# Output gates of a hybrid GLA/FNet layer: from channels on partitions to tokens on partitions, stored as 16-bit halves and reloaded by transposing transfers

## The chip, the cores and the metric

The kernel runs on one core of one Trainium2 chip. The metric is device time of one execution in microseconds (us): 1936.42 us is the median of 3 runs before the change (1936.19 to 1936.66). Engines are named as in the profile: PE (TensorE matmul), PEld (its weight loads), DVE (VectorE), ACT (ScalarE), POOL (GpSimd), SP (SyncE, which issues most DMAs).

## What is computed

One layer over 384 tokens (128 context, 256 latent) of width D = 2048, in float32. The part that matters here is the mixer:

```
def mixer(h, ...):
    proj = h @ w_in                      # q, k, v, g, decay factors, Fourier groups
    ...                                  # o: bidirectional gated linear attention (GLA)
    ...                                  # f: 2-D Fourier mixing
    gates = sigmoid(h @ w_gate + b_gate) # w_gate: 2048 x 4096
    g_a, g_b = split(gates, 2)
    merged = g_a * (o @ w_br_gla) + g_b * (f @ w_br_four)
    return merged @ w_out
```

Around it stand adaLN modulation (vectors from `w_ada`), RMSNorms and a SwiGLU FFN of 5632 hidden channels.

## The kernel before

All products keep float32 accuracy by splitting both operands in two parts of a shorter format (hi and lo) and summing three products: hi x hi, hi x lo, lo x hi. The activations stand as `hT` (tiles `A_hi`, `A_lo`): 16 blocks of 128 channels on partitions, 384 tokens along the row. Weights come in tiles of 128 x 1024 (512 KB): SP loads one into `raw` (two buffers), ACT casts it to `whi`, DVE subtracts to give `wlo` (four buffers of each). `load`, `split`, `push` and `grab` (L187 to L240) do that: each `grab` hands out the oldest ready tile, issues the load of a later one and the cast and split of the one loaded before. The order of the loads is the list `srcs` at the top.

The stages around the change, in the order of time:

- **Gates** (197 to 503 us). For each of 32 blocks of 128 gate channels `proj` (L259) takes two weight tiles; the weights stand in the array (stationary, 128 x 128) and the 384 tokens stream (moving): 48 matmuls of 384 columns into one PSUM tile `pmm` of the pool `psm` (three banks). `gate` (L839) evicts it with the bias to `gz` (ACT, L841) and stores it to DRAM as `gates_d[i]`, channels on partitions, tokens along the row. After each tile `step(sd)` runs one step of two side programs. One is `gla()`, a generator for the linear attention of four heads that goes on to its next `yield`. The other is `ada`, which streams `w_ada` through DVE (L574, two operations of 128 x 1024 per step) for the modulation vectors. Both put their work between the tiles of the main stream, on the same in-order engines. The GLA's small products use a pool of five other banks (`pss`).
- **Fourier inputs** (503 to 600 us): eight more blocks of `proj`, with `dft()` and `ada` in the side steps.
- **Merge** (600 to 761 us). The list `mix_order` interleaves eight projections for the GLA's own output gate ("o"), 16 Fourier products ("b", `four`) and 16 GLA products ("a"). A b unit takes one weight tile, whose halves DVE first adds and subtracts (`fold`, L204 and L205), then 17 short matmuls, evictions on ACT and DVE, a product with its gate and a store of y to DRAM (`four_d`). An a unit takes one tile, 24 matmuls of 384 columns, a product with its gate (L1033), the sum with the reloaded y and a split into the tiles of the next stage. Once the o units are over, a, b, a repeats. After each a or b unit `gate_of` (L962) loads the gate of a unit further on (`gates_d`, and y for a units) and applies the sigmoid to the gate of the next one (ACT, L977).
- Then the output projection, the residual and the FFN (from 761 us). In the FFN the 512-column form is used: tokens are the stationary operand, four blocks of 128 weight columns the moving one. That stage also turns tiles by splitting float32 in 16-bit halves (`apart`, L1610), transposing DMAs from ACT's queue (L1616) and joining the halves (`together`, L1620).

ACT, DVE, POOL and PE run in the order of the program. SP's order is set by the scheduler of the language, by priority.

Of the kernel before, what the change touches and what calls it, by code (L numbers as in the profile page):

```python
# [11 lines left out]
F32 = mybir.dt.float32  # L12
# [9 lines left out]
P = 128  # L22
# [75 lines left out]
def tile_step(ctx: ExitStack, tc: tile.TileContext, a, o):  # L98
# [48 lines left out]
    for i in range(XU, 8):  # L147
        srcs += two(a["w_in"], i)
    for i in range(32):
        srcs += two(a["w_gate"], i)  # L150
    for i in range(16, 24):
# [38 lines left out]
    def load(raw=None):  # L190
        n, src = next(srcs, (0, None))
        if src is not None:
            if raw is None:
                raw = wp.tile([P, G], F32, tag="raw", name="raw", bufs=2)
            SP.dma_start(raw, src)
            raws.append((raw, n in folded))
# [406 lines left out]

    gates_d = dram.tile([32, P, T], F32, name="gates_d")
    qT, kT = qk[:, 0:4, :], qk[:, 4:8, :]
# [8 lines left out]
    with ExitStack() as s:  # L614
# [23 lines left out]
        def gla():  # L638
# [10 lines left out]
            for h in range(NH):  # L649
# [9 lines left out]
                for d in range(2):  # L659
                    s0.append(pg.tile([P, 1, DV], F32, tag=f"s0{d}", name="s0"))  # L660
                    SP.dma_start(s0[d], a["s0"][d, h])
                yield
                qin, kin, kcr, kout, dec = [], [], [], [], []
# [86 lines left out]
                for c in range(2):  # L750
                    v = att[hf(c), :, c * CH : (c + 1) * CH]
                    DVE.tensor_add(v, v, am[hf(c)])
                yield
                for d in range(2):
# [82 lines left out]
        rate[0] = 1.0  # L837
        for i in range(32):
            def gate(p, i=i):  # L839
                g = pg.tile([P, T], F32, tag="gz", name="gz", bufs=2)  # L840
                ACT.activation(g, p, AF.Identity, bias=bgate[:, i : i + 1])  # L841
# [7 lines left out]
    four_d = dram.tile([KT, P, T], F32, name="four_d")  # L849
    with ExitStack() as s:  # L850
# [110 lines left out]

        def gate_of():  # L962

            u = next(gorder, None)
            if u is not None:
                b, i = u
                g = pc.tile([P, T], F32, tag="gate", name="gate", bufs=4)
                SP.dma_start(g, gates_d[i + (16 if b == "b" else 0)])
                y = None
                if b == "a":  # L970
                    y = pc.tile([P, T], F32, tag="yb", name="yb", bufs=4)
                    SP.dma_start(y, four_d[i])
                gates[u] = g, y
                raw_gates.append(g)
            if raw_gates and (u is None or len(raw_gates) > 1):
                g = raw_gates.pop(0)
                ACT.activation(g, g, AF.Sigmoid)  # L977

# [38 lines left out]
        for b, i in mix_order:  # L1017
            if b == "o":
                if i == 1:
                    gate_of()  # L1020
# [1002 lines left out]
```

## Time and profile before

| | |
|---|---|
| median of 3 runs | 1936.42 us |
| the profiled execution | 1936.08 us |
| its span, first to last instruction | 1934.3 us |
| PE, DVE, ACT busy | 99%, 85%, 55% |
| gates, from 197 to 503 us | 306 us |
| merge, from 600 to 761 us | 161 us |
| granted TensorE clock | 0.999 |

The profile is one execution taken by the hardware profiler. A row of a timeline gives the start, the duration, the engine, the source line, the operation, the tiles written and read, the shape and, in brackets, how long the engine stood idle before it and what ended that. A row of a group gives least, median and greatest duration in ns. In the windows the numbers are busy time and, in brackets, the count of each engine; the last three are the granted clock, the mean busy share of the 16 DMA engines and the GB/s that they moved. Matmuls overlap, so their durations are longer than their distance from start to start.

### The profile page before, as it was taken

How to read it: one execution, taken by the hardware profiler on the slowest of the kernel's cores; microseconds unless marked ns; L12 is line 12 of the kernel's file. 1: busy time of each engine (PE TensorE's matmuls, PEld its weight loads, DVE VectorE, ACT ScalarE, POOL GpSimd, SP SyncE). 2: the span in 40 equal slices, each digit the busy share in tenths (PEclk: the TensorE clock that was granted, in tenths of full speed). 3: DMA queues.
4: the chain of work that ended last, by engine and by line, in shares of the span. 5: the costliest groups of instructions: out<-in, count | busy, mean ns of one | idle time of the engine just before them, and what ended most of it. 6: DMA issues, size and time to landing. Idle time of an engine off the chain costs nothing.

```text
span 1934.3 us, 27954 instructions
## 1 busy us (share of the span) xinstructions
PE 1918.5 (99%) x10398; PEld 1702.5 (88%) x10398; DVE 1641.8 (85%) x2059; ACT 1069.3 (55%) x1523; POOL 145.2 (8%) x171
## 2 busy tenths in 40 slices
PE   8999999999999999999999999999999999999998
PEld 5779999999999999999988888888888888888886
DVE  5569888879776797977789999999999999988885
ACT  4233454554335655446556666766666666666555
POOL 0000000000000000002100111111111120211001
PEclk9999999999999999999999999999999999999999
DMA  9978676767754687654639696979788797969553
GB/s 389 371 263 269 228 257 219 241 219 259 256 190 145 204 287 246 218 185 154 231 98 280 155 284 151 262 170 244 191 243 207 212 230 192 252 136 253 158 199 128
DMA packets 246152, 429.12 MB, mean 222 GB/s; under 512 B 45308, under 2 KB 149948, under 8 KB 241664
## 3 DMA queue, kind: packets, MB, share of 16 engines
q1 hardware_dynamic: 199072, 386.70, 60.0%
q0 software_dynamic: 18432, 33.56, 11.3%
q10 hardware_dynamic: 28512, 7.08, 2.3%
q8 instruction: 81, 1.33, 0.3%
q14 instruction: 55, 0.45, 0.1%
HBM read 365.68 MB, written 54.53 MB: 217 GB/s over the span
## 4 chain that ended last, share of the span: by engine, by line
PE 97%; DMA 1%; DVE 1%; ACT 0%; issue 0%; SPq 0%; POOL 0%; DVEq 0%; POOLq 0%; ACTq 0%
PE pmm L257 36%; PE pgu L1539 31%; PE pdn L1539 10%; PE pds L1539 7%; PE pv L399 3%; PE pgm L382 1%; PE pf L998 1%; DMA slab<-in_w_ada 1%; PE px L417 1%; PE pmm L1253 1%; PE pf L999 1%; PE bk L1539 1%; PE po L647 1%; PE pr L582 0%; PE dl L647 0%; PE pp L881 0%
## 5 line engine op out<-in xcount | busy, mean ns | idle before, releaser
L257 PE MATMUL pmm<-A_hi,whi 128*128 128x384 f32 x1200 | 404.3, 337 | 0.0
L257 PE MATMUL pmm<-A_hi,wlo 128*128 128x384 f32 x1200 | 401.4, 334 | 0.0
L257 PE MATMUL pmm<-A_lo,whi 128*128 128x384 f32 x1200 | 401.3, 334 | 0.0
L1437 ACT CAST whi<-u 128x1024 fp32r<-128x1024 f32 x200 | 210.1, 1053 | 173.1 <-PE pds L1539 42.6
L223 ACT CAST whi<-raw 128x1024 fp32r<-128x1024 f32 x181 | 189.8, 1051 | 171.3 <-DMA raw<-in_w_gate 62.2
L1448 DVE TENSOR_TENSOR wlo<-u,whi 128x1024 fp32r<-128x1024 f32 x200 | 243.7, 1220 | 34.1 <-ACT whi L1437 32.5
L224 DVE TENSOR_TENSOR wlo<-raw,whi 128x1024 fp32r<-128x1024 f32 x179 | 217.9, 1220 | 52.5 <-ACT whi L223 49.7
L1539 PE MATMUL pgu<-whi,A_hi 128*128 128x512 f32 x640 | 249.9, 390 | 0.0
L1539 PE MATMUL pgu<-whi,A_lo 128*128 128x512 f32 x640 | 249.2, 389 | 0.0
L257 PEld LDWEIGHTS pmm<-A_hi,whi 128*128 128x128 f32 x1200 | 225.3, 188 | 2.9 <-issue 1.8
L257 PEld LDWEIGHTS pmm<-A_lo,whi 128*128 128x128 f32 x1200 | 225.4, 188 | 0.2
L257 PEld LDWEIGHTS pmm<-A_hi,wlo 128*128 128x128 f32 x1200 | 225.3, 188 | 0.0
L574 DVE SCALAR_TENSOR_TENSOR adacc<-adaw,cond,adacc 128x1024 f32<-128x1024 f32 x180 | 222.7, 1278 | 2.8 <-DMA adaw<-in_w_ada 2.5
L1437 ACT CAST whi<-raw 128x1024 fp32r<-128x1024 f32 x157 | 165.0, 1053 | 87.2 <-PE pgu L1539 27.9
L1448 DVE TENSOR_TENSOR wlo<-raw,whi 128x1024 fp32r<-128x1024 f32 x157 | 191.1, 1218 | 12.6 <-ACT whi L1437 12.2
L1539 PE MATMUL pgu<-wlo,A_hi 128*128 128x512 f32 x640 | 185.8, 389 | 0.0
L1539 PEld LDWEIGHTS pgu<-whi,A_hi 128*128 128x128 f32 x640 | 120.1, 188 | 25.9 <-issue 0.8
L1539 PEld LDWEIGHTS pgu<-wlo,A_hi 128*128 128x128 f32 x640 | 120.1, 188 | 25.1
L1539 PEld LDWEIGHTS pgu<-whi,A_lo 128*128 128x128 f32 x640 | 120.1, 188 | 24.7
L1539 PE MATMUL pgu<-whi,S 128*128 128x512 f32 x400 | 116.6, 389 | 0.0
L1672 POOL DMA_DIRECT2D sums_d<-spare x64 | 58.5, 950 | 625.3 <-ACT spare L1668 618.9
L1539 PE MATMUL pdn<-whi,hid_hi 128*128 128x512 f32 x264 | 102.8, 389 | 0.0
(410 smaller groups left out, 3302.3 us busy)
## 6 DMA issues: line engine op xcount, KB each, us to landing
adaw<-in_w_ada SPq DMA_DIRECT2D x96, 512.0 KB, 4.2
raw<-in_w_d SPq DMA_DIRECT2D x70, 512.0 KB, 5.2
slab<-in_w_ada SPq DMA_DIRECT2D x32, 1024.0 KB
raw<-in_w_gate SPq DMA_DIRECT2D x64, 512.0 KB, 4.5
raw<-in_w_g SPq DMA_DIRECT2D x48, 512.0 KB, 3.7
raw<-in_w_u SPq DMA_DIRECT2D x48, 512.0 KB, 5.2
raw<-in_w_in SPq DMA_DIRECT2D x44, 512.0 KB, 4.3
u<-in_w_u SPq DMA_DIRECT2D x40, 512.0 KB, 7.1
```

The costliest lines, as they stand in the source:

```text
L223: ACT.copy(hi, raw)
L224: sub = lambda: eng.tensor_sub(lo, raw, hi.bitcast(F32))
L257: PE.matmul(dst, w[wi][:, k * n + n0 : k * n + n0 + P], x[xi][:, k0 + k, :], start=first and k == 0 and j == 0, stop=last and k == kts - 1 ...
L382: PE.matmul(pgv[q : q + 32, :], spad[:, k, :], slab[k // (KT // 2)][:, k % (KT // 2), :], start=k < 4, stop=k >= KT - 4,)
L399: PE.matmul(pv[2 * t + g], hT[x_][:, kb, t * P : (t + 1) * P], w_[:, g * 512 : (g + 1) * 512], start=kb == 0 and j == 0, stop=kb == KT - 1 ...
L417: PE.matmul(px, w_[:, u * P : (u + 1) * P], hT[x_][:, kb, :], start=j == 0, stop=j == 2)
L574: DVE.scalar_tensor_tensor(acc[:, c, :], w, cond[:, k, c : c + 1], acc[:, c, :], op0=ALU.mult, op1=ALU.add,)
L647: PE.matmul(dst, w[wi], x[xi], start=first and j == 0, stop=last and j == 2)
L1437: ACT.copy(hi, src)
L1448: DVE.tensor_sub(lo, src, hi.bitcast(F32))
L1539: PE.matmul(dst, stat[x_][m], mov(w[w_], m), start=first and w_ == m == x_ == 0, stop=last and w_ == m == 1, skip_group_check=any(more),)
L1672: POOL.dma_start(sums_d[k], u, accum_op=ALU.add)
```

## The change

- **Matmuls of the gates.** Tokens become the stationary operand and 512 gate channels the moving one. A group q of 512 channels takes eight weight tiles m, each with 2 x 128 input channels for 512 gate channels (its load reads runs of 256 floats). Per tile there are 3 token tiles x 2 input blocks x 3 products = 18 matmuls of 512 columns. The group's result stands in three PSUM banks, one for each token tile, which are all that the pool `psm` has.
- **Eviction and store.** After tile m=7 of a group ACT copies each bank, read as 16-bit numbers, so that the 128 low halves and the 128 high halves of each channel block stand in rows of their own (`gpl`, three buffers), and SP stores it: tokens on partitions.
- **Reload.** In the merge a transposing DMA from SP's queue brings 256 of these 16-bit columns back as 128 channels x (2 halves x 384 tokens). ACT then joins the halves into `gate` (new copy, L1007) and applies the sigmoid, now with the bias (L1010). Reloads are issued four units ahead (`gate_load`), y as before.
- **Side steps.** `gla()` loses three of its yields per head: after the loads of the initial states, after the merge of the attention masks, and after the output product of token tile 0. At m=6 and m=7 of each group only `ada` is stepped.
- `gates_d` becomes eight DRAM tensors and `four_d` sixteen.

```diff
-    for i in range(32):
-        srcs += two(a["w_gate"], i)
+    for q in range(8):
+        for m in range(8):
+            src = a["w_gate"][4 * q : 4 * q + 4, m // 4, :, 256 * (m % 4) : 256 * (m % 4) + 256]
+            srcs.append(src.rearrange("n p x -> p n x"))
...
                     SP.dma_start(s0[d], a["s0"][d, h])
-                yield
...
                     DVE.tensor_add(v, v, am[hf(c)])
-                yield
...
                     ACT.activation(junk, po, AF.Square, accum_out=ss[:, t, h : h + 1])
-                    yield
+                    if t:
+                        yield
...
-        for i in range(32):
-            def gate(p, i=i):
-                g = pg.tile([P, T], F32, tag="gz", name="gz", bufs=2)
-                ACT.activation(g, p, AF.Identity, bias=bgate[:, i : i + 1])
-                SP.dma_start(gates_d[i], g)
-
-            proj(psm, hT, gate, sd)
+        for q in range(8):
+            pt = [psm.tile([P, 512], F32, tag="mm", name="pgt") for _ in range(3)]
+            for m in range(8):
+                w = [x.rearrange("p (n k c) -> p n k c", n=4, k=2) for x in grab()]
+                for t in range(3):
+                    ts = slice(t * P, (t + 1) * P)
+                    for k in range(2):
+                        for j, (wi, xi) in enumerate(((0, 0), (0, 1), (1, 0))):
+                            PE.matmul(
+                                pt[t], hT[xi][:, 2 * m + k, ts], w[wi][:, :, k, :],
+                                start=m == k == j == 0, stop=m == 7 and k == 1 and j == 2,
+                            )
+                    if m == 7:
+                        pl = pg.tile([P, 2 * 512], U16, tag="gpl", name="gpl", bufs=3)
+                        ACT.copy(
+                            pl.rearrange("p (n h c) -> p n h c", n=4, h=2),
+                            pt[t].bitcast(U16).rearrange("p (n c h) -> p n h c", n=4, h=2),
+                        )
+                        SP.dma_start(gates_d[q][ts, :], pl)
+                step(ada if m in (6,7,) else sd)
...
+        def gate_load():
+
+            u = next(gorder, None)
+            if u is not None:
+                b, i = u
+                n = i + (16 if b == "b" else 0)
+                pl = pc.tile([P, 2 * T], U16, tag="gpl", name="gpl", bufs=4)
+                SP.dma_start(
+                    pl.rearrange("p (h t) -> p h t", h=2), gates_d[n // 4][:, 256 * (n % 4) : 256 * (n % 4) + 256],
+                    transpose=True,
+                )
+                raw_gates.append((u, pl))
...
+        def gate_of():
+
+            if raw_gates:
+                u, pl = raw_gates.pop(0)
+                b, i = u
+                n = i + (16 if b == "b" else 0)
+                g = pc.tile([P, T], F32, tag="gate", name="gate", bufs=3)
+                y = ys.pop(u, None)
+                y_load()
+                ACT.copy(
+                    g.bitcast(U16).rearrange("p (x h) -> p h x", h=2), pl.rearrange("p (h x) -> p h x", h=2),
+                )
+                ACT.activation(g, g, AF.Sigmoid, bias=bgate[:, n : n + 1])
                 gates[u] = g, y
-                raw_gates.append(g)
-            if raw_gates and (u is None or len(raw_gates) > 1):
-                g = raw_gates.pop(0)
-                ACT.activation(g, g, AF.Sigmoid)
+            gate_load()
```

Three places show what moves in the engines' own order. ACT among the gates, before, in the first head (`eb`, `ki`, `ko` are the GLA's decay factors, `att` its attention tile):

```order
L706 ACTIVATE ko<-sx 128x256
L223 CAST whi<-raw 128x1024
L841 ACTIVATE gz<-pmm,bgate 128x384
L223 CAST whi<-raw 128x1024 x2
L841 ACTIVATE gz<-pmm,bgate 128x384
L755 COPY att<-cr 64x3x64 x2
```

and in the change, around the end of the first group:

```order
L707 ACTIVATE ko<-sx 128x256
L589 COPY adacc<-pr 128x256
L225 CAST whi<-raw 128x1024 x2
L853 COPY gpl<-pgt 128x1024 x3
L225 CAST whi<-raw 128x1024 x2
L755 COPY att<-cr 64x3x64 x2
```

One eviction for every two casts has become three copies in a row once in eight casts, directly behind the cast that tile m=7 issues.

PE in the same stage, before, where the output products of token tiles 0 and 1 of a head begin (`ap` is the split attention, `vr` the values, `qp` the split queries, the last `part` the split states):

```order
L257 MATMUL pmm<-A_lo,whi 128x384
L257 MATMUL pmm<-A_hi,wlo 128x384
L647 MATMUL po<-vr,ap 128x256 x3
L647 MATMUL po<-part,qp 128x256 x6
L257 MATMUL pmm<-A_hi,whi 128x384
```

and in the change:

```order
L847 MATMUL pgt<-whi,A_lo 128x512
L847 MATMUL pgt<-wlo,A_hi 128x512
L649 MATMUL po<-vr,ap 128x256 x6
L649 MATMUL po<-part,qp 128x256 x6
L847 MATMUL pgt<-whi,A_hi 128x512
```

The three products of token tile 0, which stood one weight tile earlier, are now in the same step as those of tile 1; the last three of the six products with `part` read the state of direction 1.

ACT in the merge, before, where a, b, a repeats (`ws` is a folded weight tile of a b unit, `fd` a b unit's eviction, `yb` the sum of an a unit):

```order
L1002 COPY fd<-pf 128x194 x2
L223 CAST whi<-ws 128x1024
L977 ACTIVATE gate<-gate 128x384
L223 CAST whi<-raw 128x1024
L283 CAST A_hi<-yb 128x384
L977 ACTIVATE gate<-gate 128x384
```

and in the change:

```order
L1037 COPY fd<-pf 128x194 x2
L225 CAST whi<-ws 128x1024
L1007 COPY gate<-gpl 128x2x384
L1010 ACTIVATE gate<-gate,bgate 128x384
L225 CAST whi<-raw 128x1024
L285 CAST A_hi<-yb 128x384
L1007 COPY gate<-gpl 128x2x384
L1010 ACTIVATE gate<-gate,bgate 128x384
```

A joining copy stands ahead of each sigmoid, and so ahead of the next weight cast.

More of the change, by code (lines that the diff above doesn't have):

```diff
@@ L194, in load @@
                 raw = wp.tile([P, G], F32, tag="raw", name="raw", bufs=2)
-            SP.dma_start(raw, src)
+            SP.dma_start(raw if len(src.shape) == 2 else raw.rearrange("p (n x) -> p n x", n=src.shape[1]), src)
             raws.append((raw, n in folded))
@@ L601, in ada_rest @@
                     DVE.tensor_mul(mh, mh, bc(norms[:, w1, :]))
-    gates_d = dram.tile([32, P, T], F32, name="gates_d")
+    gates_d = [dram.tile([T, 2 * 512], U16, name=f"gates_d{n}") for n in range(8)]
     qT, kT = qk[:, 0:4, :], qk[:, 4:8, :]
@@ L837, in tile_step @@
         rate[0] = 1.0
-        for i in range(32):
-            def gate(p, i=i):
-                g = pg.tile([P, T], F32, tag="gz", name="gz", bufs=2)
-                ACT.activation(g, p, AF.Identity, bias=bgate[:, i : i + 1])
-                SP.dma_start(gates_d[i], g)
-            proj(psm, hT, gate, sd)
+        for q in range(8):
[18 more added lines that the diff above has]
+                step(ada if m in (6,7,) else sd)
         for _ in gl:
             pass
-    four_d = dram.tile([KT, P, T], F32, name="four_d")
+    four_d = [dram.tile([P, T], F32, name=f"four_d{n}") for n in range(KT)]
     with ExitStack() as s:
@@ L960, in tile_step @@
         gorder = iter([u for u in mix_order if u[0] != "o"])
-        def gate_of():
+        def gate_load():
             u = next(gorder, None)
@@ L966, in gate_of, with y_load @@
                 b, i = u
[L967 to L972, printed above, removed]
+                n = i + (16 if b == "b" else 0)
[5 more added lines that the diff above has]
+                raw_gates.append((u, pl))
+        ys = {}
+        def y_load():
+            if raw_gates and raw_gates[0][0][0] == "a":
+                u = raw_gates[0][0]
+                ys[u] = pc.tile([P, T], F32, tag="yb", name="yb", bufs=4)
+                SP.dma_start(ys[u], four_d[u[1]])
+        def gate_of():
[10 more added lines that the diff above has]
+                ACT.activation(g, g, AF.Sigmoid, bias=bgate[:, n : n + 1])
                 gates[u] = g, y
-                raw_gates.append(g)
-            if raw_gates and (u is None or len(raw_gates) > 1):
-                g = raw_gates.pop(0)
-                ACT.activation(g, g, AF.Sigmoid)
+            gate_load()
         def gcol(p, i):
@@ L1018, in tile_step @@
             if b == "o":
-                if i == 1:
-                    gate_of()
+                if i < 2:
+                    gate_load()
+                    if i == 0:
+                        gate_load()
                 proj(psm, hT, lambda p: gcol(p, i), sd)
```

## The prediction, on record before the changed kernel ran

> **What bounds the kernel now.** I read the page's busy shares first, then its chain that ended last.
>
> ```profile
> span 1934.3 us, 27954 instructions
> PE 1918.5 (99%) x10398; PEld 1702.5 (88%) x10398; DVE 1641.8 (85%) x2059; ACT 1069.3 (55%) x1523; POOL 145.2 (8%) x171
> PE 97%; DMA 1%; DVE 1%; ACT 0%; issue 0%; SPq 0%; POOL 0%; DVEq 0%; POOLq 0%; ACTq 0%
> ```
>
> The chain runs over PE for 97% of the span, so a microsecond of matmul starts saved is a microsecond gained, unless another engine falls behind. Busy time of PE is no pace, because matmuls overlap. Next come the windows by stage: the gates (197 to 503) and, after the Fourier inputs, the merge (600 to 761), where the gates are used.
>
> ```profile
> core 0: us, PE busy (x) PEld busy (x) DVE busy (x) ACT busy (x) POOL busy (x), PEclk, DMA share, GB/s
> 197.00:503.00 306.00, 306.00 (x1986) 301.43 (x1985) 260.81 (x331) 148.07 (x249) 1.87 (x6) 1.00 0.72 237
> 600.00:690.00 90.00, 89.47 (x558) 88.97 (x557) 69.11 (x135) 58.30 (x85) 0.00 (x0) 1.00 0.64 205
> 690.00:761.00 71.00, 70.81 (x424) 70.49 (x423) 61.56 (x113) 38.26 (x66) 0.00 (x0) 1.00 0.83 276
> ```
>
> PE has holes only in the merge (0.53 + 0.19 us). The clock is full throughout. ACT is half idle among the gates and 65% busy in the first part of the merge; DVE is 85 to 87% busy in both. The pace of the matmuls is read from start to start in the timeline: an old gate form, a 512-column form of the FFN whose moving operand is cut like the new one (four blocks of 128), and the 512-column form of the V projection, which moves one block.
>
> ```profile
> 304.18 0.33 PE L257 MATMUL pmm<-A_hi,whi 128*128 128x384 f32 x1
> ...
> 307.99 0.33 PE L257 MATMUL pmm<-A_lo,whi 128*128 128x384 f32 x1
> ```
> ```profile
> 1199.84 0.39 PE L1539 MATMUL pgu<-whi,A_lo 128*128 128x512 f32 x1
> ...
> 1201.20 0.39 PE L1539 MATMUL pgu<-whi,left 128*128 128x512 f32 x1
> ```
> ```profile
> 137.14 1.55 PE L399 MATMUL pv<-wlo,A_hi 128*128 128x512 f32 x6
> 138.53 0.85 PE L399 MATMUL pv<-whi,A_lo 128*128 128x512 f32 x3
> ```
>
> 22 steps in 3.81 us are 173.2 ns for 384 columns; 6 steps in 1.36 us are 226.7 ns for 512; in the V projection 6 steps in 1.39 us are 231.7 ns.
>
> **The matmuls.** Before, 32 blocks x 48 = 1536 matmuls of 384 columns; after, 8 groups x 8 tiles x 18 = 1152 of 512. Both stream 589,824 columns, so only the part that each matmul costs beyond its columns can shrink. 1536 x 173.2 ns = 266.0 us; 1152 x 226.7 ns = 261.2 us: **-4.8 us**. At the V projection's pace it would be 266.9 us, +0.9. I take -4.8, because the FFN form has the same cut of the moving operand and the same order of halves; the sum goes by these rows. The Trainium skill ("TensorE: Matmul & The Clock Gate", "Wait — 56ns, not 53.3ns?") puts a warm step at N over 2.4 GHz plus about 2.5 ns, 162.5 and 215.8 ns, by which the saving would be only 1.0 us. The trace disagrees: its rows lie some 11 ns above that in both forms.
>
> **The turn of the banks.** Before, each block filled one of three PSUM banks and its eviction had two blocks' time. Now all three banks are full at the end of a group, and the next group begins in the first of them. Tile m=7 starts its bank-0 matmuls at T and ends them at T+1.36; bank 0 is wanted again at T+4.08 (18 x 226.7 ns), banks 1 and 2 1.36 us apart behind it. The copy that splits 16-bit halves is not in the trace from PSUM; the FFN's split from SBUF and the old eviction bound it.
>
> ```profile
> L841 ACT ACTIVATE gz<-pmm,bgate x32: 572/582/585, 205.6 to 500.9; 128x384 f32<-128x384 f32 x32
> ```
> ```profile
> L1613 ACT COPY ep<-ep x18: 1037/1040/1047, 1049.4 to 1786.8; 128x1024 uint16<-128x1024 uint16 x18
> L1622 ACT COPY ep<-ep x18: 1348/1356/1360, 1066.3 to 1805.4; 128x1024 uint16<-128x1024 uint16 x18
> ```
>
> I take 1.04 us. An idle ACT would free bank 0 at T+2.4. But in ACT's queue the cast of m=7's load stands ahead, and it often waits for its DMA:
>
> ```profile
> 373.44 0.33 PE L257 MATMUL pmm<-A_hi,whi 128*128 128x384 f32 x1
> ```
> ```profile
> 377.45 1.05 ACT L223 CAST whi<-raw 128x1024 fp32r<-128x1024 f32 x1 [5.68 <-DMA raw<-in_w_gate]
> ```
> ```profile
>   DMA raw<-in_w_gate: 62.2, 29
> ```
>
> That tile began at 373.44 and its cast at 377.45, 4.0 us later. The same at m=7 would put the copy at T+5.1 to T+6.1, a stall of 2.0 us; eight turns bound the cost at 0 and 16 us. In all, 29 casts waited 62.2 us, 2.1 us each, in 64 tiles. A cast up to T+2 costs nothing, and at m=6 and m=7 the change steps only the modulation stream, so DVE and ACT have less in front. I take 0.15 us per turn, +1.2. ACT's total among the gates goes from 32 x 0.58 = 18.6 to 24 x 1.04 = 25.0 us, which its idle half covers. Loads in runs of 1 KB are not in these stages; a down projection load (runs of 2 KB) lands in 5.2 us, a gate load in 4.5:
>
> ```profile
> raw<-in_w_d SPq DMA_DIRECT2D x70, 512.0 KB, 5.2
> raw<-in_w_gate SPq DMA_DIRECT2D x64, 512.0 KB, 4.5
> ```
>
> 0 to 0.7 us of landing; weights are cast three tiles ahead, so nothing reaches PE through them. It enters the term above.
>
> **The linear attention steps.** Twelve steps go, three per head. Two of the merged places add no wait on PE; the third does. The output products of token tiles 0 and 1 now follow the state products of direction 1 by one tile, not by one and two:
>
> ```profile
> 390.83 0.88 PE L647 MATMUL dl<-vr,part 128*128 128x256 f32 x6
> ```
> ```profile
> 395.42 0.47 DVE L781 SCALAR_TENSOR_TENSOR S<-s,dc,dl 128x256 f32<-128x256 f32 x1
> 396.37 0.42 DVE L284 TENSOR_TENSOR part<-S,part 128x256 fp32r<-128x256 f32 x1 [0.47 <-ACT part L283]
> ```
>
> DVE reaches the state only 4.6 us after its product began, and the split is ready at 396.79, 5.96 us after. The changed PE arrives after 0.72 (six products, up to 391.55) + 4.08 (tile) + 9 products at 0.12 = 5.9 us. So some 0.1 us per head, +0.4 to 0.6 with jitter; bounds -1 (fewer breaks) and +5 (one 1.22 us weight split more ahead, four heads). I take +0.6.
>
> **The merge.** Each of 32 gates gets one more ACT copy: 768 halves per partition, interleaved. Three quarters of L1613 and L1622 are 0.78 and 1.02 us; I take 1.0. It stands ahead of the sigmoid and so ahead of the next weight cast. Where ACT idles anyway it costs nothing; where the pipeline is thin it is passed on:
>
> ```profile
> 689.35 1.05 ACT L223 CAST whi<-ws 128x1024 fp32r<-128x1024 f32 x1 [2.75 <-DVE ws L205]
> 690.31 0.52 ACT L977 ACTIVATE gate<-gate 128x384 f32<-128x384 f32 x1
> 691.11 1.05 ACT L223 CAST whi<-raw 128x1024 fp32r<-128x1024 f32 x1 [0.28 <-DMA raw<-in_w_br_gla]
> ```
> ```profile
> 692.38 0.36 PE L999 MATMUL pf<-edT,wlo 128*128 128x194 f32 x1 [0.19 <-DVE wlo L224]
> ```
> ```profile
> 708.13 0.68 DVE L204 TENSOR_TENSOR ws<-raw 128x512 f32<-128x512 f32 x1
> ```
> ```profile
> 718.38 0.69 DVE L204 TENSOR_TENSOR ws<-raw 128x512 f32<-128x512 f32 x1 [0.57 <-DMA raw<-in_w_br_four]
> ```
>
> At 692 PE already waits for weights: no margin. The copy at 690.31 would move the cast at 691.11 by 0.7 us. Before that cluster some 0.7 us more arrive from the b units ahead: +1.4 around 676 to 703. Later, three units (two GLA, one Fourier) recur:
>
> ```profile
> 705.42 0.36 PE L257 MATMUL pmm<-o_hi,whi 128*128 128x384 f32 x1
> ```
> ```profile
> 716.17 0.36 PE L257 MATMUL pmm<-o_hi,whi 128*128 128x384 f32 x1
> ```
> ```profile
> 713.79 1.05 ACT L223 CAST whi<-raw 128x1024 fp32r<-128x1024 f32 x1 [0.62 <-DMA raw<-in_w_br_gla]
> ```
> ```profile
> 715.07 1.22 DVE L224 TENSOR_TENSOR wlo<-raw,whi 128x1024 fp32r<-128x1024 f32 x1
> ```
>
> PE needs 10.75 us for them. DVE (708.13 to 718.38) needs 10.25, 0.57 of it idle. Two copies stand ahead of the cast at 713.79; the first arrives as 0.7 us, the second loses 0.6 in that cast's gap, so it moves by 1.1 and ends at 715.9, and the split at 715.07 moves by 0.8. DVE's cycle becomes 10.5 to 11.1 us (the idle 0.57 kept or not): about PE's own. At up to 0.35 us for six such cycles, 0 to 2 us, I take +1.0. The bounds are 0 (all in ACT's gaps) and 18 us (the 18 of 32 sigmoids behind which ACT now goes on without a gap of 1 us). Sum **+2.4**.
>
> **The transposing reloads.** 27 transposes of 256 KB stand in the FFN:
>
> ```profile
> q1 hardware_dynamic: 199072, 386.70, 60.0%
> q10 hardware_dynamic: 28512, 7.08, 2.3%
> ```
> ```profile
> L1616 ACTq DMA_TRANSPOSE ep<-ep x18: 1249/1376/2142, 1050.5 to 1787.8; - x18
> ```
> ```profile
> DMA to landing us min/median/max: 5.3/8.9/11.7
> ```
>
> 0.023 x 1934.3 / 27 = 1.65 us of all engines each, so 1.2 us for 192 KB, where a plain load at q1's rate takes 0.6. 32 x 0.6 = 20 us, most of it over the merge's 161 us, lift DMA shares of 0.64 and 0.83 by about 0.12, to 0.76 and 0.95: nearly full in the second part, where the reloads could come late. Landing in at most 11.7 us meets a load issued three units (about 10.75 us) ahead of its use. SP issues each in 1.2 to 2.1 us instead of 0.42, and weight loads queue behind it; yet SP mostly waits for DVE. I take 0; bounds 0 and +3 (ten landings late by 0.3 us). If the four reloads of lead were not enough, ACT would stand at the copy.
>
> **The sum.** -4.8 + 1.2 + 0.6 + 2.4 + 0 = **-0.6 us**. The profiled execution took 1936.08 us (span 1934.3 and 1.8 around it), 0.3 below the median of 1936.42; less 0.6 that is **1935.5 us**. About 0.2% (3.9 us) is what a measurement of this kernel can tell from no change.
>
> **Rivals.**
> - Everything that is added hides: 1936.08 - 4.8 = 1931.3. For it: ACT's idle half, 1.7 us between a bank's last matmul plus copy and its next use. Against it: PE's waits near 690. Chance 0.25.
> - ACT becomes the pace of the merge (slower): after 676, where PE has no lead left, some 12 of the copies run straight into the next weight cast; at 1.0 us each, +12 in place of +2.4, 1945.0. It decides as soon as DVE's three-unit cycle passes PE's 10.75 us by more than it now falls short (0.5). Chance 0.17.
> - The new matmuls run at the V projection's 231.7 ns: +0.9 + 4.2 = 1941.2. Against it: the cut of the operand. Chance 0.08.
> - The change does not save what it says. The two paces differ by 53.5 ns for 128 columns, 0.418 ns per column, which leaves 12.7 ns for each matmul beyond its columns. If four fifths of that went with the columns after all, the 384 matmuls less would save 384 x 2.5 ns = 1.0 us: -1.0 + 4.2 = 1939.3. Against it: both paces were measured. Chance 0.04. The rule of the Trainium skill named above gives this time too.
>
> **How the numbers follow.** The forecast, with stalls of 1 to 8 us in all, has 0.46 (1932.3 to 1939.3). Faster by over 0.2% is the first rival: 0.25. Slower is the second and third, 0.25. The rest, 0.50, lies within. The range from 1931.0 to 1943.0 takes in the first rival and the third and cuts the second in its upper part.
>
> **What would show it.** Start-to-start 226 to 227 ns in the gates, and that stage about 4 us shorter. At each turn the first matmul of a group waits for the split copy (L853) under 0.5 us; waits near 2 us would make the second term wrong. ACT's join copies (L1007) near 1.0 us, PE waiting for weight splits around 680 to 720 by 1 to 4 us in all; none there gives the first rival, 10 us the second. Landings of the reloads over 11 us with ACT idle at L1007 would prove the last term wrong.

## The result, and the profile after

The changed kernel takes 1950.05 us (median of 6 runs, 1946.97 to 1953.17) against 1936.14 us before (6 runs): a ratio of 1.0071, 95% interval 1.0058 to 1.0083, so it is 13.9 us slower. The forecast was 1935.5 us in a range of 1931.0 to 1943.0. The profiled execution took 1949.21 us; its span is 13.1 us longer than before.

The head of the page, the chain of work that ended last, and the three windows of before, now of the changed kernel:

```profile
span 1947.4 us, 27135 instructions
PE 1921.1 (99%) x10014; PEld 1653.6 (85%) x10014; DVE 1642.7 (84%) x2059; ACT 1109.4 (57%) x1547; POOL 144.9 (7%) x171
PE 89%; DMA 4%; DVE 3%; ACT 3%; issue 1%; SPq 0%; POOL 0%; DVEq 0%; ACTq 0%; POOLq 0%
```
```profile
197.00:503.00 306.00, 300.38 (x1572) 247.21 (x1572) 254.82 (x322) 150.23 (x237) 1.85 (x6) 0.99 0.71 228
600.00:690.00 90.00, 90.00 (x565) 89.76 (x564) 67.41 (x129) 71.05 (x95) 0.00 (x0) 1.00 0.68 198
690.00:761.00 71.00, 65.42 (x381) 63.00 (x380) 53.86 (x102) 50.32 (x74) 0.00 (x0) 1.00 0.88 227
```

The busy shares hardly moved, which shows how little they tell here. The chain did: PE fell from 97% of it to 89%, and DMA, DVE and ACT came in. PE now has 5.6 us of holes in the gates' window and 5.6 us in the second one of the merge. DVE is less busy there than before, so no engine became the bound by its load; PE waits on chains.

Two marks on PE divide the loss: the time from the start of the span to the first product of the Fourier inputs (`pp`, behind the gates), and the stretch from the first Fourier product of the merge (`pf`) to the first FFN product (`pgu`).

```profile
533.82 0.33 PE L895 MATMUL pp<-cd,xc 128*128 128x65 f32 x2
...
606.18 0.42 PE L1033 MATMUL pf<-edT,whi 128*128 128x388 f32 x1
...
981.80 0.39 PE L1576 MATMUL pgu<-whi,A_hi 128*128 128x512 f32 x1
```
```profile
527.64 0.33 PE L881 MATMUL pp<-cd,xc 128*128 128x65 f32 x2
...
600.01 0.42 PE L998 MATMUL pf<-edT,whi 128*128 128x388 f32 x1
...
968.65 0.39 PE L1539 MATMUL pgu<-whi,A_hi 128*128 128x512 f32 x1
```

The first is the changed kernel, the second the one before. The gates lost 6.2 us, the merge 7.0 (375.6 against 368.6); the FFN lost nothing.

**In the gates** the matmuls themselves run as forecast: the median from start to start is 227 ns. Two kinds of wait ate the gain. The first is the turn of the banks. Around one turn, ACT's rows with PE's:

```profile
464.80 1.04 ACT L225 CAST whi<-raw 128x1024 fp32r<-128x1024 f32 x1 [4.23 <-DMA raw<-in_w_gate]
...
465.87 2.84 ACT L853 COPY gpl<-pgt 128x1024 uint16<-128x1024 uint16 x3
```
```profile
466.93 0.68 PE L847 MATMUL pgt<-whi,A_hi 128*128 128x512 f32 x1 [2.05 <-ACT gpl L853]
467.41 0.63 PE L847 MATMUL pgt<-whi,A_lo 128*128 128x512 f32 x1
467.83 0.63 PE L847 MATMUL pgt<-wlo,A_hi 128*128 128x512 f32 x1
...
470.39 0.45 PE L847 MATMUL pgt<-wlo,A_hi 128*128 128x512 f32 x1
```

The cast waited 4.23 us for its load, the copies stood behind it, and the new group's first matmul started 2.21 us late. Then eight matmuls stand 426 ns apart instead of 227. That is the clock; the same again at 293 us, in the windows of the changed kernel:

```profile
293.00:297.00 4.00, 4.00 (x13) 3.09 (x12) 4.00 (x8) 1.77 (x4) 0.00 (x0) 0.57 0.45 141
...
467.00:471.00 4.00, 4.00 (x11) 3.15 (x12) 3.91 (x5) 2.89 (x4) 0.00 (x0) 0.57 0.95 328
```

The granted clock is 0.57 over these 4 us. Each time it adds some 1.6 us (8 x 0.2) to a wait that is already over. The three turns with a wait lost 0.64, 0.94 and 2.21 us, the slow matmuls behind the last 1.65.

The second wait is in the linear attention. The decay products `bT` need a split (`lah`, `lal`) at the end of a chain that ACT begins with `la`, read from the products `z`. In the second head, before and in the change:

```profile
281.35 0.52 PE L667 MATMUL z<-cg 98*128 98x256 f32 x3
...
282.97 0.87 ACT L675 ACTIVATE la<-z 128x512 f32<-128x512 f32 x2
...
288.89 0.96 DVE L284 TENSOR_TENSOR lal<-la,lah 128x768 fp32r<-128x768 f32 x1 [0.96 <-ACT lah L283]
...
290.03 0.22 PE L692 MATMUL bT<-cg,lah 128*128 128x128 f32 x1
```
```profile
280.93 0.60 PE L668 MATMUL z<-cg 98*128 98x256 f32 x3
...
283.60 1.05 ACT L225 CAST whi<-raw 128x1024 fp32r<-128x1024 f32 x1 [1.20 <-DMA raw<-in_w_gate]
284.56 0.86 ACT L676 ACTIVATE la<-z 128x512 f32<-128x512 f32 x2
...
290.46 0.96 DVE L286 TENSOR_TENSOR lal<-la,lah 128x768 fp32r<-128x768 f32 x1 [0.95 <-ACT lah L285]
290.48 0.33 PE L693 MATMUL bT<-cg,lah 128*128 128x128 f32 x1 [0.77 <-ACT lah L285]
291.48 0.33 PE L693 MATMUL bT<-cg,lal 128*128 128x128 f32 x1 [0.67 <-DVE lal L286]
```

Before, the split ended 0.18 us ahead of its use, and in the two heads after it 0.18 and 0.19. There was no wait to see and no room either. Now three heads wait: 2.9 us in all, with 1.56 us of slow matmuls behind one of them. The shorter tiles are the smaller part of it: two of them take 8.16 us in place of 8.31, and 0.15 us is still within the room. Nor did the chain get longer: from the start of `la` to the end of `lal` it takes 6.9 us in both kernels. It begins later. Before, `la` started 1.10 us after the end of `z` in these heads. In the change it starts 3.03 us after it in the second head, because the casts ahead of it on ACT waited for their loads, and 1.57 us after it in the third, where the copy `krs`, one removed yield nearer, stands ahead too. In the fourth, ACT comes to it only behind a turn's copies and the cast after them.

The sum of the gates: -4.8 + 3.8 + 1.65 + 2.9 + 1.56 = +5.1; the other 1.1 us lie in steps that grew by less than 0.2 us each, among them 0.34 us at `z`.

**In the merge** PE waits at the second matmul of the b units, 6.7 us in all, most of it 1.1 to 1.8 us in each of four cycles. SP's queue and DVE around one of them, in the change and before:

```profile
711.00 1.23 DVE L226 TENSOR_TENSOR wlo<-raw,whi 128x1024 fp32r<-128x1024 f32 x1 [0.59 <-ACT whi L225]
711.29 1.06 ACT L1007 COPY gate<-gpl 128x768 uint16<-128x768 uint16 x1
712.38 1.21 SPq L983 DMA_TRANSPOSE gpl<-gates_d  x1
713.78 0.43 SPq L996 DMA_DIRECT2D yb<-four_d  x1
...
714.31 0.37 SPq L197 DMA_DIRECT2D raw<-in_w_br_four  x1
...
718.41 0.69 DVE L206 TENSOR_TENSOR ws<-raw 128x512 f32<-128x512 f32 x1 [1.69 <-DMA raw<-in_w_br_four]
```
```profile
702.82 1.22 DVE L224 TENSOR_TENSOR wlo<-raw,whi 128x1024 fp32r<-128x1024 f32 x1
...
704.06 0.33 SPq L195 DMA_DIRECT2D raw<-in_w_br_four  x1
```
```profile
722.82 0.36 PE L1034 MATMUL pf<-edT,wlo 128*128 128x194 f32 x1 [1.24 <-DVE wlo L226]
```

Before, the split freed the raw buffer at 704.03 and SP issued the next Fourier load 0.03 us later. Now the buffer is free at 712.22 and the load goes out at 714.31, 2.1 us late: ahead of it in SP's order stands a reload that waits for the joining copy to free its own buffer, then takes 1.21 us to issue. Of the 2.1 us, 0.16 are the last of that wait, 1.21 the issue, and the rest the y load behind it. The view of SP's waits from 676 to 760 us has it as its first row:

```profile
SPq L983 <- ACT gate L1010: 21.7, 12, 3.2
```

One trip through the two raw buffers is a loop: load 4.44 us, fold 1.33, cast 0.96, joining copy 1.07, sigmoid 0.53, cast 1.06, split 1.23, SP's delay 2.09, the next load; 12.7 us from 701.61 to 714.31. Before it was 9.6 to 10.6 us in the last three cycles, within PE's 10.75.

### The profile page after: what moved, and what is told of

Same layout as the page of the kernel before. It is cut to its first block, busy times and chain, and to the rows that moved or that the text cites. A ratio compares the mean times of both kernels' runs of the same rounds, so it can differ in the third digit from the quotient of the medians.

```text
span 1947.4 us, 27135 instructions
## 1 busy us (share of the span) xinstructions
PE 1921.1 (99%) x10014; PEld 1653.6 (85%) x10014; DVE 1642.7 (84%) x2059; ACT 1109.4 (57%) x1547; POOL 144.9 (7%) x171
## 4 chain that ended last, share of the span: by engine, by line
PE 89%; DMA 4%; DVE 3%; ACT 3%; issue 1%; SPq 0%; POOL 0%; DVEq 0%; ACTq 0%; POOLq 0%
PE pgu L1576 31%; PE pmm L259 19%; PE pdn L1576 10%; PE pgt L847 10%; PE pds L1576 7%; PE pv L401 3%; PE pgm L384 1%; DMA raw<-in_w_gate 1%; DMA slab<-in_w_ada 1%; DMA raw<-in_w_br_four 1%; PE px L419 1%; PE pmm L1290 1%; ACT whi L225 1%; PE pf L1033 1%; DVE adacc L576 1%
## 5 line engine op out<-in xcount | busy, mean ns | idle before, releaser
L259 PE MATMUL pmm<-A_hi,whi 128*128 128x384 f32 x688 | 231.4, 336 | 0.0
L259 PE MATMUL pmm<-A_lo,whi 128*128 128x384 f32 x688 | 230.2, 335 | 0.0
L259 PE MATMUL pmm<-A_hi,wlo 128*128 128x384 f32 x688 | 230.0, 334 | 0.0
L1485 DVE TENSOR_TENSOR wlo<-raw,whi 128x1024 fp32r<-128x1024 f32 x157 | 191.1, 1218 | 12.8 <-ACT whi L1474 12.4
L847 PE MATMUL pgt<-whi,A_hi 128*128 128x512 f32 x384 | 152.7, 398 | 3.3 <-ACT gpl L853 3.3
L847 PE MATMUL pgt<-whi,A_lo 128*128 128x512 f32 x384 | 151.2, 394 | 0.0
L847 PE MATMUL pgt<-wlo,A_hi 128*128 128x512 f32 x384 | 150.9, 393 | 0.0
L259 PEld LDWEIGHTS pmm<-A_hi,whi 128*128 128x128 f32 x688 | 129.2, 188 | 1.1 <-issue 1.0
L259 PEld LDWEIGHTS pmm<-A_lo,whi 128*128 128x128 f32 x688 | 129.2, 188 | 0.7 <-DVE A_lo L286 0.5
L259 PEld LDWEIGHTS pmm<-A_hi,wlo 128*128 128x128 f32 x688 | 129.1, 188 | 0.0
```

The costliest lines, as they stand in the source:

```text
L259: PE.matmul(dst, w[wi][:, k * n + n0 : k * n + n0 + P], x[xi][:, k0 + k, :], start=first and k == 0 and j == 0, stop=last and k == kts - 1 ...
L847: PE.matmul(pt[t], hT[xi][:, 2 * m + k, ts], w[wi][:, :, k, :], start=m == k == j == 0, stop=m == 7 and k == 1 and j == 2,)
L1485: DVE.tensor_sub(lo, src, hi.bitcast(F32))
```

## The experiments

All ran five rounds or more beside the kernel before (medians 1935.96, 1936.89 and 1936.64 us in the three groups). The stretches are of each kernel's one profiled execution.

| kernel | median us | start to first pp | first pf to first pgu |
|---|---|---|---|
| before | 1936.14 | 527.6 | 368.6 |
| the change | 1950.05 | 533.8 | 375.6 |
| e1, reloads two units ahead | 1950.77 | 533.0 | 376.8 |
| e2, plain reloads on SP | 1945.73 | 529.1 | 375.2 |
| e3, old steps | 1946.40 | 531.2 | 376.1 |
| e4, copy ahead of the cast | 1945.69 | 530.6 | 376.0 |
| e5, merge weights from POOL | 1947.25 | 531.4 | 374.0 |
| e6, no joining copy | 1944.23 | 532.4 | 371.2 |
| e7, e3 and e4 | 1944.38 | 529.7 | 374.9 |
| e8, plain reloads from POOL | 1946.42 | 531.3 | 372.3 |
| e10, one yield more | 1947.53 | 530.3 | 376.5 |
| e11, joining copy on POOL | 1947.24 | 525.5 | 383.7 |
| e9, three causes mended | 1933.94 | 525.1 | 369.6 |

e1, e2, e5, e6 and e8 leave the gates alone, yet their first stretch lies anywhere from 529.1 to 533.0 us. That is the scatter of the turns and of the clock behind them. So verdicts on the gates go by the waits in a trace, not by this column. The waits scatter too: in these five and in the change, those at `bT` add up to 1.6 to 2.9 us and those at the turns to 3.7 to 5.0. The last column has the same flaw. In e3, e4, e7 and e10, which leave the merge alone, it lies between 374.9 and 376.5, and in e2, e5 and e11 the clock fell to half within it:

```profile
743.00:746.00 3.00, 3.00 (x13) 3.00 (x13) 2.76 (x5) 2.97 (x5) 0.00 (x0) 0.50 0.56 176
```
```profile
687.00:693.00 6.00, 4.95 (x18) 4.96 (x19) 4.06 (x10) 5.96 (x9) 0.53 (x1) 0.50 0.57 152
```

The first is e2, the second e5. Set against the same matmuls before the change, the slow ones cost 1.6 us in e2, 2.7 in e5 and 3.3 in e11, and none in the change.

### e1: does the reload's place decide?

```diff
                 if i < 2:
                     gate_load()
-                    if i == 0:
-                        gate_load()
```

> The reloads are issued two units ahead instead of three, with the same four buffers, so that no reload has to wait for the joining copy of the unit just before. Measured on the stretch from the first Fourier product of the merge (pf) to the first FFN matmul (pgu): 368.6 us before, 375.6 us with the change. Theory A (SyncE's queue: the reload waits there for ScalarE's copy, 44.8 us in all between 600 and 760 us, and the weight loads queue behind it): those waits fall under 10 us and the stretch is 2 to 4 us shorter. Theory B (the prediction's: the joining copies hold up the weight casts on ScalarE): within 0.7 us of 375.6. Theory C (the 1.21 us that each transposing issue occupies SyncE): the waits go, and the stretch is at most 1 us shorter.

376.8 us, but nothing was tested: the scheduler put the reloads back in nearly the same places (six of them moved behind one GLA weight load each). SP's waits in the same window:

```profile
SPq L983 <- ACT gate L1010: 21.0, 12, 3.1
```

### e2 and e8: kind of transfer, or queue?

```diff
-                SP.dma_start(
-                    pl.rearrange("p (h t) -> p h t", h=2), gates_d[n // 4][:, 256 * (n % 4) : 256 * (n % 4) + 256],
-                    transpose=True,
-                )
+                src = gates_d[n // 4][:, 256 * (n % 4) : 256 * (n % 4) + 256]
+                SP.dma_start(pl.rearrange("p (t x) -> p t x", t=3), src.rearrange("(t p) x -> p t x", t=3))
```

In e8 the last line says `POOL.dma_start`. In both, the joining copy reads its halves in the order of the plain transfer.

> The same bytes are reloaded by a plain transfer in place of the transposing one, in the same place of SyncE's order; the gates come back untransposed, so the merge multiplies by wrong numbers. Stretch from the first pf to the first pgu, 375.6 us with the change. Theory C (1.21 us of issue on SyncE, against about 0.4 for a plain one): 3 to 5 us shorter. Theory A (the wait for the copy, which stays): 0.5 to 1.5 us shorter. Theory B (ScalarE's copies): no change within 0.7 us.

> The reloads are plain transfers from GpSimd's queue (the gates come back untransposed, so the merge multiplies by wrong numbers); nothing of them is left on SyncE, and the joining copies stay. Stretch from the first pf to the first pgu: 375.6 us with the change, 375.2 with plain reloads on SyncE. Theory A (waits on SyncE for the joining copy, whatever the kind of transfer): the Fourier weight loads are issued within 0.5 us of a free buffer, the loop is about 10.3 us and the stretch 370 to 371. Theory B (the copies on ScalarE): 374 to 376.

A plain transfer on SP gives 375.2, or 373.6 without the slow matmuls: less than theory C's 3 to 5 us. Its issue takes 0.37 us in place of 1.21, yet four of the Fourier loads still go out 1.2 to 2.4 us late. SP's waits:

```profile
SPq L984 <- ACT gate L1005: 24.2, 16, 3.6
SPq L994 <- DMA four_d<-y: 6.4, 4, 2.6
```

The reload still goes out only when the copy has ended, 0.15 us after the raw buffer is free; but in three of the four cycles what then holds the Fourier load longest is the y load behind the reload, which waits for the store of its own y. So a shorter issue alone does not free the queue. That the issue had no part in the delay is not shown, since another wait took its place.

The same transfers from POOL's queue give 372.3. Three of the five loads from 685 us on leave within 0.4 us of a free buffer, and the others 1.5 and 1.9 us late behind the y loads. That is 3.3 us shorter than in the change, less than the 5 expected; one wait of 1.9 us of another kind, at 766 us, stands in this trace alone.

### e5: the weights on another queue

```diff
     raws, ready = [], []
+    queue = [SP]
...
-            SP.dma_start(raw if len(src.shape) == 2 else raw.rearrange("p (n x) -> p n x", n=src.shape[1]), src)
+            queue[0].dma_start(raw if len(src.shape) == 2 else raw.rearrange("p (n x) -> p n x", n=src.shape[1]), src)
...
+        queue[0] = POOL
         gates, raw_gates = {}, []
...
         split_act(*late.pop())
+        queue[0] = SP
```

> The weight loads of the merge are issued from GpSimd's queue; the transposing reloads, y and the stores stay on SyncE. The load of a Fourier weight tile was issued 0.03 us after its buffer came free before the change, and 2.1 us after it with the change. Stretch from the first pf to the first pgu, 375.6 us with the change, 368.6 before. Theory A (one loop through the two raw buffers: load, fold, cast, joining copy, cast, split, SyncE's delay, next load, 12.4 us in all against PE's 10.75): without the 2.1 us of delay the loop is 10.3 us plus what a GpSimd issue costs, the waits of the b units fall from 6.7 to under 2 us and the stretch is 4 to 6 us shorter. Theory B (the joining copies alone): 0 to 1 us shorter.

374.0: 1.6 us shorter, not 4 to 6. But 2.7 us of it are the slow matmuls from 687 to 693 us shown above; without them it would be 371.3, which is 4.3 us shorter. The waits that recur are gone; from 691 us on the loop takes 10.7 to 11.1 us with the joining copies in it.

```profile
711.37 1.23 DVE L227 TENSOR_TENSOR wlo<-raw,whi 128x1024 fp32r<-128x1024 f32 x1 [0.63 <-ACT whi L226]
...
712.89 0.53 POOL L198 DMA_DIRECT2D raw<-in_w_br_four  x1 [4.38 <-DVE wlo L227]
```

What stays is one pair of waits near 687 us (1.9 and 1.8 us), where the slow matmuls begin: the Fourier load issued at 675.56, beside the 3 MB of the next stage's `xT`, was folded 8.1 us later; in every kernel that has it on SP the same load took 5.4 to 5.6.

### e6: without the joining copy

```diff
-                ACT.copy(
-                    g.bitcast(U16).rearrange("p (x h) -> p h x", h=2), pl.rearrange("p (h x) -> p h x", h=2),
-                )
-                ACT.activation(g, g, AF.Sigmoid, bias=bgate[:, n : n + 1])
+                ACT.activation(g, pl[:, T : 2 * T].bitcast(mybir.dt.bfloat16), AF.Sigmoid, bias=bgate[:, n : n + 1])
```

> The joining copy is left out; the sigmoid reads the upper halves alone, as 16-bit floats, so the gates have some three digits. SyncE's queue stays as it is with the change. Stretch from the first pf to the first pgu, 375.6 us with the change. Theory A (the loop of 12.4 us, in which the copy is 1.07 us and SyncE's delay 2.1 us): the loop is 11.2 to 11.4 us, still 0.5 over PE's 10.75, and five to six cycles lose 2 to 4 us in place of 6.7: 3 to 4.5 us shorter. Theory B (the copies alone): all of the loss goes, 6 to 7 us shorter. If SyncE alone decides: within 1 us.

371.2: 4.4 us shorter, as the loop has it (3 to 4.5), not the whole 7. SP's delay fell with it, to 0.8 to 1.4 us, since the sigmoid now frees the reload's buffer and stands where the copy stood. Copy and delay are two links of one loop, so their shares can't be added up: taking out either one brings the loop near PE's pace.

### e3, e4 and e7: the two waits of the gates

e3 restores the three yields and steps the linear attention at every m:

```diff
                     SP.dma_start(s0[d], a["s0"][d, h])
+                yield
...
                     DVE.tensor_add(v, v, am[hf(c)])
+                yield
...
-                    if t:
-                        yield
+                    yield
...
-                step(ada if m in (6,7,) else sd)
+                step(sd)
```

e4 moves the next cast, and e7 has both edits:

```diff
-                w = [x.rearrange("p (n k c) -> p n k c", n=4, k=2) for x in grab()]
+                w = [x.rearrange("p (n k c) -> p n k c", n=4, k=2) for x in (take() if m == 7 else grab())]
...
                         SP.dma_start(gates_d[q][ts, :], pl)
+                        if t == 0:
+                            push()
```

> The linear attention is stepped as before the change: its three yields per head are back, and m=6 and m=7 step it too. Time from the start to the first pp matmul: 527.6 us before, 533.8 us with the change. Theory D (the removed yields put the decay products bT too close behind their split): the waits at bT (2.9 us, and 1.6 us of slow matmuls behind one of them) go and the time is 530 or less. Rival (late weight casts, which push the decay chain on ScalarE wherever it stands): waits of 1 to 3 us at bT stay and the time lies within 1.5 us of 533.8. Both: the waits at the turn of the banks stay, 2 to 6 us.

> At tile m=7 the next weight cast (with its load and its split) is put behind the copy of the first bank instead of ahead of it. Time from the start to the first pp matmul, 533.8 us with the change. Theory E (the late cast ahead of the copy makes the turn of the banks late: 3.8 us of waits and some 1.8 us of slow matmuls behind one of them): the matmuls of a new group wait under 0.3 us in all and the time is 4 to 6 us shorter. Rival (the copies themselves, 1.01 us each, are too slow for three banks): 2 us or more of waits stay. If the cast is wanted earlier than that, the matmuls wait for wlo instead, and nothing is gained.

> Both edits of the gates together: the linear attention is stepped as before the change, and at tile m=7 the next cast stands behind the copy of the first bank. Time from the start to the first pp matmul: 533.8 us with the change, 527.6 before, 531.2 and 530.6 with either edit alone. If the two are independent (waits at bT 2.9 us and at the turn of the banks 3.8 us, each with up to 1.8 us of slow matmuls behind it): 524 to 526.5, below the kernel before by the 4.8 us of the matmuls less 1 to 3 us that stays. If one wait only takes the place of the other: 529 or more. The merge stays within 1 us of 375.6.

In e3 the waits at `bT` fall from 2.9 to 0.95 us, below all of the scatter but not to 0, so the removed yields were not the whole cause. The turns cost 4.5 us there, 3.2 of them at one turn where no cast waited for its load. In e4 the turns cost 0.62 us, and `bT` 3.5. Together (e7) they do not add up:

```profile
464.62 0.59 PE L848 MATMUL pgt<-whi,A_hi 128*128 128x512 f32 x1 [2.33 <-ACT gpl L854]
```

Here ACT's copy stood behind a split of the attention state (3.19 us of waiting for DVE), because with the old steps that work runs at m=6 and m=7 again. The same wait of 3.19 us stands ahead of that turn in e3. The change's rule for m=6 keeps just this away from the copies.

### e10: one yield between split and product

```diff
                 split_act(lah, lal, la)
                 yield
+                yield
                 if h == 0:
                     yield
-                    yield
```

> The changed kernel with one yield more per head (three of four heads), between the split lal and bT, and nothing else. Time from the start to the first pp matmul, 533.8 us with the change. If the waits at bT come from a chain of 8.5 us that had 0.18 us to spare before and has none in two tiles of 4.08 us: the waits at bT are 0, and the time 529 to 531. If the chain runs late by whatever is ahead of it: waits of 1 us or more stay. The waits at the turns stay in both, 3 to 5 us and perhaps slow matmuls behind one.

No matmul of `bT` waits any more, so what was missing is room ahead of `bT`; the time to the first pp is 530.3. The chain still begins late: `la` starts 2.70 and 4.02 us after `z` in the second and third head, behind casts that waited for loads, and one tile more of room hides it. So the run does not tell a chain that is too short from one that begins late; that it begins late is read from the rows, and no run took the late casts away alone. The turns still cost 6.9 us, at four of seven.

### e9 and e11: mended

e9 has e4's edit, e10's yield, and e5's queue with a later switch; tile m=7 steps the linear attention again:

```diff
-                step(ada if m in (6,7,) else sd)
+                step(ada if m == 6 else sd)
...
         for b, i in mix_order:
+            if (b, i) == ("b", 9):
+                queue[0] = POOL
```

The load that was late in e5 stays on SP that way. e11 has the gates of e9; in its merge only the joining copy is moved:

```diff
-                ACT.copy(
+                POOL.tensor_copy(
                     g.bitcast(U16).rearrange("p (x h) -> p h x", h=2), pl.rearrange("p (h x) -> p h x", h=2),
                 )
```

> Three causes mended together, all of the computation kept: at tile m=7 the next cast stands behind the first bank's copy; one more yield of the linear attention lies between the split of the decay (lal) and its products bT, and m=7 steps it again to make room; and from the ninth Fourier product on the merge's weight loads come from GpSimd's queue, behind the one load that met the 3 MB of the next stage's loads. Time from the start to the first pp matmul: 533.8 us with the change, 527.6 before; if the waits at bT and at the turns are gone with their slow matmuls, 523 to 525. Stretch from the first pf to the first pgu: 375.6 with the change, 368.6 before; if the loop through the raw buffers is at PE's pace, 369 to 371. Both give 1932 to 1935 us, faster than the kernel before. If new waits take their place, 1938 or more.

> The mended gates of the run before last, but the merge's weights on SyncE as in the change, and the joining copy on GpSimd, which is idle there, in place of ScalarE. Stretch from the first pf to the first pgu, 375.6 us with the change, 371.2 without the joining copy. If GpSimd's copy takes under 3 us and only ScalarE's 1.07 us in the loop matter: 371 to 373. If the reloads now wait on SyncE for a later copy, or GpSimd's copies slow DVE: 376 or more.

e9 takes 1933.94 us: 0.9989 of before, 95% interval 0.9981 to 0.9998. It is the fastest of all. Its gates end 2.6 us earlier than before the change, its merge is 0.9 us longer. The windows:

```profile
197.00:503.00 306.00, 305.69 (x1618) 253.68 (x1617) 261.96 (x332) 153.81 (x241) 1.86 (x6) 1.00 0.74 237
600.00:690.00 90.00, 89.50 (x553) 88.74 (x553) 70.19 (x137) 72.36 (x98) 2.87 (x5) 1.00 0.72 212
690.00:761.00 71.00, 70.72 (x419) 69.81 (x418) 58.16 (x105) 57.47 (x83) 9.50 (x18) 1.00 0.97 259
```

PE is without holes again in the second part of the merge. ACT still makes all 32 copies and is 81% busy there, more than in the change. So ACT's load did not limit the merge.

e11's merge is 383.7 us, 8 longer. DVE's split, in the groups of 690 to 761 us:

```profile
L226 DVE TENSOR_TENSOR wlo<-raw,whi 128x1024 fp32r<-128x1024 f32 x13 | 24.4, 1874 | 2.6 <-ACT whi L225 2.6
```
```profile
L226 DVE TENSOR_TENSOR wlo<-raw,whi 128x1024 fp32r<-128x1024 f32 x13 | 15.9, 1225 | 6.9 <-ACT whi L225 6.9
```

First e11, then the change. The same operation takes 1874 ns on average in place of 1225; in e11 it takes 1.21 to 1.23 us where no copy of POOL overlaps it, and up to 2.04 where one does. Of the 8 us, 3.3 are slow matmuls behind waits.

## Why the prediction was wrong, point by point

- **The matmuls (-4.8): right.** From the first to the last matmul of the gates, the sum of the steps from start to start is 269.1 us for the 1536 before and 264.3 for the 1152 in e9: -4.8. The V projection's pace did not come true. Nor did the saving of 1.0 us by the rule of the Trainium skill ("TensorE: Matmul & The Clock Gate", "Wait — 56ns, not 53.3ns?").
- **The turn of the banks (+1.2): the mechanism was right, the size was not.** Three of seven turns waited, 3.8 us behind the cast that "often waits for its DMA", where 0.15 us per turn was taken; with the cast behind the first copy (e4) it was 0.6. The missing term is the clock: a wait of 2 us cost 1.65 more.
- **The linear attention (+0.6): the failed step.** "Two of the merged places add no wait on PE" stands in the prediction without a row. The +0.6 was priced at the third place, by the state S, whose products do not wait in the change. The wait came at `bT`, 2.9 us and 1.56 of slow matmuls. The rows of before held the risk: 0.18 us between split and product in three heads, on an engine where the casts and copies ahead of that chain were about to move. I looked only at waits that existed.
- **The merge (+2.4) and the reloads (0): wrong apart, because they act together.** The copy takes 1.07 us (1.0 was taken) and the issue 1.21 (1.2 to 2.1), both as priced; landing took 4.4 us, far from 11.7. What failed is "SP mostly waits for DVE": a reload that waits on SP for ACT, its issue and the y load behind it hold back the weight load. Copy and delay lengthen one loop from about 10.3 to 12.4 us and more, and PE, which needs 10.75, waits once per cycle: 6.7 us in all. I had priced the copy against DVE's cycle and the issue against SP's idle time, and never closed the loop.
- **The rivals.** The slower one (ACT paces the merge) had the right place and sign, even the right condition, "as soon as DVE's three-unit cycle passes PE's 10.75 us", and 0.17 of the chance. Its cause was half of it: without the copies (e6) 4.4 of the 7.0 us go, but in e9 ACT makes the same copies and PE waits 0.3 us in the whole second part. The chances of 0.50 and 0.25 for no change and for faster had no room for two stages that both lose.

What stays open: why the changed kernel's executions lie 6 us apart where those of before lie within 1.1. The waits at the turns move with the landing of loads, and the clock drops behind some of them only; that this is the whole spread was not shown.

## What to carry to other kernels

A chain that ends 0.2 us ahead of its use costs nothing today and is the first to break when anything ahead of it moves or the stage around it gets shorter: list such margins, not only waits. In a ring of few buffers add up every link, the issuing queue's in-order waits included, and compare the sum with PE's time for one trip; a link's own duration against its engine's idle share says nothing. A queue that issues both prefetches and reloads should not hold the one whose buffer is freed late ahead of the one that is urgent; here another queue for the weights, with three small edits of order, turned 13.9 us lost into 2.7 gained.

## What the runs showed of the hardware

- **The clock drops behind short waits, but not behind each.** In the change it was 0.57 over a window of 4 us, with eight matmuls 426 ns apart in place of 227, after PE idled 2.05 us, and again after 0.77 and 0.67 us within 1.8. In the same trace it stayed at 1.00 through the merge, whose waits reach 1.53 us, and in e10 after 3.14 us:

```profile
388.20 0.50 PE L847 MATMUL pgt<-whi,A_hi 128*128 128x512 f32 x1 [3.14 <-ACT gpl L853]
```
```profile
388.00:392.00 4.00, 3.80 (x17) 3.15 (x18) 4.00 (x5) 1.98 (x3) 0.00 (x0) 1.00 0.96 326
```

 The Trainium skill ("TensorE: Matmul & The Clock Gate", "What's actually happening") describes a free-running window of about 3.4 us, which agrees with the length of the drop (eight times 426 ns) and would make the drop a matter of where the wait falls in it. Its advice in "Why this matters for your kernels", no idle gaps over about 3 us, is too generous by these rows: 2 us were enough.
- **POOL's copies and DVE's operations slow each other.** With the copies on POOL the split took 1874 ns on average in place of 1225; one copy of 768 halves per partition took 1.06 to 2.03 us on POOL and 1.07 on ACT.
